# Scaling and biasing the accumulators in the norm stage, and shifting squares and differences between VectorE, ScalarE and GpSimd in an encoder layer

## The chip, the cores and the metric

The kernel runs on one core of one Trainium2 chip. The metric is the device time of one execution in microseconds (us), as the median of several runs. The engines are named as the profile names them: PE is TensorE (matmul), DVE is VectorE, ACT is ScalarE, POOL is GpSimd, SP is SyncE, which issues most of the DMAs. A line number such as L1143 is a line of the kernel before; where the changed kernel's numbers are meant, the text says so.

## What is computed

One encoder layer on 1024 tokens of width 1024, all in fp32. Token mixing (dilated window attention and Fourier mixing, joined by gates) comes first; then a norm, a squared-ReLU MLP of inner width 4096, and a second norm. The part that matters here is:

```python
h = _layer_norm(ALPHA * h + mix, ln1_g, ln1_b)
ff = square(relu(h @ w_up + b_up)) @ w_down + b_down
h = _layer_norm(ALPHA * h + ff, ln2_g, ln2_b)
```

The second sum is `ALPHA * h + b_down + (the down projection's product)`. The first two terms depend on the first norm's output alone, so a kernel is free to form them at any time between the first norm and the last product.

## The kernel before

**Arithmetic.** A number is split into a high part (a cast to fp32r by ACT, L63) and a low part (the difference, by DVE, L64; the function is `split`). A product is three matmuls, high by high, high by low and low by high (`mm3`, L75 to L77). PE therefore has three matmuls of 128x512 for each product, and each operand costs one ACT cast and one DVE difference. The large projections use a scheme of seven block products in place of eight, so the operands are sums and differences of blocks, and the results are joined afterwards.

**Order.** The program is written engine by engine in one Python text; a scheduler with a limited number of buffers for each tag (U 31, wr 3, w 10, S 8, PT 6) decides the order in each engine's queue, and each queue runs strictly in that order. An instruction that waits holds all that is behind it on its engine. `issue_after` keeps a DMA from being issued ahead of another one.

**Norm stage (about 850 to 985 us).** It is the loop over `hf` (two halves of 512 tokens), `c` (two column halves) and `t` (four tiles of 128 tokens). L947 adds the scaled input to the product, L832 to L846 make the statistics, L953 and L954 scale a tile z of 128x1024, and L955 writes it to the DRAM scratch `accd`. Later the tile is transposed by PE (`transposed`, L867), copied out of PSUM by ACT (L872) into `h1t`, and `token_blocks` (L901 to L911) forms the block sums for the up projection on DVE, with ACT casts and DVE differences after each (tiles `tb`).

**Up projection (to about 1276 us).** There are 16 pairs of 128-column blocks; pairs 0 and 1 are done without the block scheme (WHOLE = 2), pairs up to 4 begin early (START = 5). `block_steps` makes the seven products p1 to p7 of a pair. `keep` copies a product out of PSUM (ACT, L976), `joined` adds a second one (DVE, L989), and `done` applies ReLU with the bias on ACT (L980) and then squares: on ACT (L982) for pairs below START, on DVE (L984) for the others. The result q has one of eight S buffers. In p3 four sums and differences of q run on POOL (L1044 to L1050), each followed by a DMA from POOL's queue (L996) to the scratch `qd`; other results go to `qd` from ACT's queue.

**Down projection (about 1276 to 1560 us).** The accumulators `acc` are eight tiles of 128x1024, read back from `accd` (L1133). Eight instructions on DVE (L1135) turn each into ALPHA * acc + b_down; the row b_down is loaded for it (L825, called at L1130). For each of the groups (2,4), (6,4), (10,4) and (14,2) `add_up` goes through seven block products. `a_block` loads a block of q from `qd` into one of three wr buffers (L1139), casts it on ACT (L1141) and forms the low part (L1143); which engine forms it depends on the name of the block and the group:

```python
sub = (nc.vector if name in ("A11", "A12") or pair < WHOLE + 4 and name in ("S2", "S3")
       else nc.gpsimd).tensor_tensor
```

`b_block` forms sums of the weight blocks on DVE (L1163 to L1172) and splits them. `product` runs the matmuls and then adds each PSUM bank into acc on DVE (L1197, the eviction). A bank is used again by a later product, so PE waits for its eviction.

Of the kernel before, what the change touches and what calls it, by code (L numbers as in the profile page):

```python
# [14 lines left out]
ALU = mybir.AluOpType  # L15
# [3 lines left out]
ALPHA = 2 ** 0.25  # L19
# [9 lines left out]
def tile_hybrid_layer(ctx, tc, a, out):  # L29
# [5 lines left out]
    nc = tc.nc  # L35
# [23 lines left out]
    def ps(tag):  # L59
        return psum.tile([128, 512], F32, tag=tag, bufs=PB[tag], name=nm("p" + tag))  # L60
# [586 lines left out]
    for gp in range(2):  # L647
# [5 lines left out]
        for d in range(8):  # L653
# [5 lines left out]
            h, l = cwh[d // 2][:, d % 2], cwl[d // 2][:, d % 2]  # L659
# [162 lines left out]
    def row(name):  # L822
        t = U([128, 1024], name=name)
        src = a[name]
        nc.sync.dma_start(t, bass.AP(tensor=src.tensor, offset=src.offset, ap=[[0, 128], [1, 1024]]))  # L825
        return t
# [22 lines left out]
        nc.vector.tensor_scalar(q[:, 5:6], r, also, None, op0=ALU.mult)  # L849
        return q[:, 0:1], r, q[:, 5:6]  # L850

    g1, b1 = row("ln1_g"), row("ln1_b")
    bup = const.tile([128, 32], F32, name="bup")
    nc.sync.dma_start(bup, a["b_up"])
    accd = dram.tile([8, 128, 1024], F32, name="accd")
# [5 lines left out]
    def transposed(hf, t, h):  # L861
        tc_ = slice(128 * t, 128 * t + 128)
        for q in range(2):
            p = ps("s")
            for i in range(4):
                k = 4 * q + i
                nc.tensor.transpose(p[:, 128 * i:128 * i + 128], h[:, 128 * k:128 * k + 128], ident)  # L867
            for i in range(2):
                dp = 2 * q + i
                if t == 0:  # L870
                    raw[hf, dp] = U([128, 2, 512], name="h1t")
                nc.scalar.copy(  # L872
                    raw[hf, dp][:, :, tc_], p[:, 256 * i:256 * i + 256].rearrange("p (d n) -> p d n", d=2))
        if hf == 0 and t == 3:
            plain_block("B11", 0)
        if hf == 1 and t == 3:
            token_blocks(1)

    def plain_block(name, d0):
        for dp in range(d0, d0 + 2):  # L880
            h_, l_ = U([128, 2, 512], F32R, "tb"), U([128, 2, 512], F32R, "tb")
            split(raw[0, dp], h_, l_)
            for v, x in zip(TB[name], (h_, l_)):
                v.append(x)
# [42 lines left out]
    WHOLE, START = 2, 5  # L927
# [3 lines left out]
    for hf in range(2):  # L931
        zs = [U([128, 1024], name="z") for _ in range(4)]
        stats = []
        for c in range(2):
            s = slice(512 * c, 512 * c + 512)
            w = [weights(a["wout"][c, u], [128, 2, 512]) for u in range(4)]
            for t in range(4):
                p = ps("mm")
                tc_ = slice(128 * t, 128 * t + 128)
                xr = tmp([128, 512])  # L940
                nc.sync.dma_start(xr, a["xr"][512 * hf + 128 * t:512 * hf + 128 * t + 128, s])
                for k in range(8):
                    mm3(p, mgh[hf, k // 2][:, k % 2, tc_], mgl[hf, k // 2][:, k % 2, tc_],
                        w[k // 2][0][:, k % 2], w[k // 2][1][:, k % 2], k == 0, k == 7)
                if len(late) > 1 or late and c == 0:
                    transposed(*late.pop(0))
                nc.vector.scalar_tensor_tensor(zs[t][:, s], xr, ALPHA, p, op0=ALU.mult, op1=ALU.add)  # L947
                if c == 0:
                    stats.append(norm_stats(zs[t], (0,)))
                else:  # L950
                    h = zs[t]
                    mu, r = norm_scale(norm_stats(h, (1,), stats[t]))
                    nc.vector.scalar_tensor_tensor(h, h, mu, g1, op0=ALU.subtract, op1=ALU.mult)  # L953
                    nc.vector.scalar_tensor_tensor(h, h, r, b1, op0=ALU.mult, op1=ALU.add)  # L954
                    nc.sync.dma_start(accd[4 * hf + t], h)  # L955
                    late.append((hf, t, h))


# [1 line left out]
    def block_steps(pair):  # L960
        w = WB[pair]
        ba, bb = bup[:, 2 * pair:2 * pair + 1], bup[:, 2 * pair + 1:2 * pair + 2]
        bank, part = {}, {}

        def product(x, y, b, tag=None):
            first = tag is not None
            if first:
                bank[b] = ps(tag)
            for k in range(4):
                ks = slice(128 * k, 128 * k + 128)  # L970
                h_, l_ = (v[k // 2][:, k % 2] for v in TB[y])
                mm3(bank[b], w[x][:, 0, ks], w[x][:, 1, ks], h_, l_, first and k == 0, k == 3, True)

        def keep(name, b="x", make=tmp):
            part[name] = make([128, 512], name="part")
            nc.scalar.copy(part[name], bank[b])  # L976

        def done(src, bias, r=None):
            r, q = r or tmp([128, 512]), half([128, 512], name="q")
            nc.scalar.activation(r, src, AF.Relu, bias=bias)  # L980
            if pair < START:
                nc.scalar.activation(q, r, AF.Square)  # L982
            else:
                nc.vector.tensor_tensor(q, r, r, op=ALU.mult)  # L984
            return q

        def joined(name, b, bias):
            t = part[name]
            nc.vector.tensor_tensor(t, t, bank[b], op=ALU.add)  # L989
            return done(t, bias, t)  # L990

        pool = nc.gpsimd.tensor_tensor
        q = {}

        def save(name, t):
            (nc.gpsimd if name[0] == "S" else nc.scalar).dma_start(qd[pair - WHOLE, NAMES.index(name)], t)  # L996

        def plain(i, c, t):
            nc.scalar.dma_start(qp[2 * pair + i, :, 512 * c:512 * c + 512], t)

        def whole(c):
            for i, (x, y, bias) in enumerate((("A11", "A12", ba), ("A21", "A22", bb))):
                if c == 0:
                    product(x, "B11", "y", "pt")
                    keep(i, "y", half if pair else tmp)
                    product(y, "B21", "y")
                    plain(i, 0, done(bank["y"], bias))
                else:
                    product(x, "T1", "y", "pt")
                    product(y, "B22", "y")  # L1010
                    plain(i, 1, joined(i, "y", bias))

        def p1():
            product("A11", "B11", "x", "mm")
            keep("r1")

        def p2():
            product("A12", "B21", "y", "pt")
            q[11] = joined("r1", "y", ba)
            save("A11", q[11])  # L1020

        def p6():
            product("S2", "T2", "x")
            keep("r2")

        def p5():
            product("S1", "T1", "z", "s")

        def p7():
            product("S3", "T3", "x")  # L1030
            keep("r3")
            q[22] = joined("r3", "z", bb)
            save("A22", q[22])

        def p4():
            product("A22", "T4", "x")
            q[12] = done(bank["x"], bb)
            save("A12", q[12])

        def p3():  # L1040
            product("S4", "B22", "z")
            q[21] = joined("r2", "z", ba)
            s3 = half([128, 512], name="q")
            pool(s3, q[11], q[21], op=ALU.subtract)  # L1044
            save("S3", s3)
            pool(q[21], q[21], q[22], op=ALU.add)
            save("S1", q[21])
            pool(q[11], q[21], q[11], op=ALU.subtract)
            save("S2", q[11])
            pool(q[12], q[12], q[11], op=ALU.subtract)  # L1050
            save("S4", q[12])

        return dict(c0=lambda: whole(0), c1=lambda: whole(1), p1=p1, p2=p2, p3=p3, p4=p4, p5=p5, p6=p6, p7=p7)
# [73 lines left out]
        r0 = b_raws(WHOLE, 4)  # L1127
    acc = []
    with tc.issue_after(last):
        bdn = row("b_down")  # L1130
        for t in range(8):
            acc.append(U([128, 1024], name="acc"))
            nc.sync.dma_start(acc[t], accd[t])  # L1133
    for t in range(8):
        nc.vector.scalar_tensor_tensor(acc[t], acc[t], ALPHA, bdn, op0=ALU.mult, op1=ALU.add)  # L1135

    def a_block(name, pair):
        r = wr([128, 2, 512])
        load[0] = nc.sync.dma_start(r, qd[pair - WHOLE:pair - WHOLE + 2, NAMES.index(name)].rearrange("b p n -> p b n")).ins  # L1139
        h_, l_ = U([128, 2, 512], F32R), U([128, 2, 512], F32R)  # L1140
        nc.scalar.copy(h_, r)  # L1141
        sub = (nc.vector if name in ("A11", "A12") or pair < WHOLE + 4 and name in ("S2", "S3") else nc.gpsimd).tensor_tensor
        sub(l_, r, h_.bitcast(F32), op=ALU.subtract)  # L1143
        return h_, l_

# [183 lines left out]
```

## Time and profile before

| quantity | value |
| --- | --- |
| median of 3 runs | 1610.8 us (1607.35 to 1611.06) |
| profiled execution | 1611.52 us |
| its span in the profile | 1609.7 us |
| mean granted clock of PE | 0.991 |
| instructions in the span | 20761 |
| read from HBM, written | 159.30 MB, 57.54 MB |
| POOL busy | 268.1 us (17%) |

The profile's span covers the instructions of the engines; the time of the execution has 1.8 us more around it. The profiled execution is 0.7 us above the median. In the profile's groups a line gives engine, operation, output and input tiles, the number of instructions, their busy time and mean length in ns, and after the second bar how long the engine stood idle right before them and for whom. A list of waits gives, for each instruction that waited, the engine and line that it waited for, the total, the number of times and the longest. In the windows the granted clock is the share of full speed that PE was given, and the DMA share is how busy the 16 DMA engines were.

### The profile page before, as it was taken

How to read it: one execution, taken by the hardware profiler on the slowest of the kernel's cores; microseconds unless marked ns; L12 is line 12 of the kernel's file. 1: busy time of each engine (PE TensorE's matmuls, PEld its weight loads, DVE VectorE, ACT ScalarE, POOL GpSimd, SP SyncE). 2: the span in 40 equal slices, each digit the busy share in tenths (PEclk: the TensorE clock that was granted, in tenths of full speed). 3: DMA queues.
4: the chain of work that ended last, by engine and by line, in shares of the span. 5: the costliest groups of instructions: out<-in, count | busy, mean ns of one | idle time of the engine just before them, and what ended most of it. 6: DMA issues, size and time to landing. Idle time of an engine off the chain costs nothing. (4 is left out here: it accounts for less than half of the span.)

```text
span 1609.7 us, 20761 instructions
## 1 busy us (share of the span) xinstructions
PE 1563.2 (97%) x7636; PEld 1274.8 (79%) x7636; DVE 1035.8 (64%) x1708; ACT 647.0 (40%) x1299; POOL 268.1 (17%) x282
## 2 busy tenths in 40 slices
PE   8999999999999999899899999999999989999997
PEld 6788888888988777888788887888888778888885
DVE  7565544144422533947676786477778997878878
ACT  5333334255433645523322355554444443333312
POOL 0000000000100000300000000133333542525414
PEclk9999999999999999999999999999999999999998
DMA  6433333421411232536655533344437763535502
GB/s 187 162 131 110 106 105 121 150 103 54 138 40 61 74 124 75 174 107 186 185 168 161 168 123 131 118 151 146 154 132 261 259 200 124 193 94 170 170 14 92
DMA packets 104224, 218.21 MB, mean 136 GB/s; under 512 B 21128, under 2 KB 30792, under 8 KB 104122
## 3 DMA queue, kind: packets, MB, share of 16 engines
q1 hardware_dynamic: 69498, 167.81, 32.5%
q10 hardware_dynamic: 28320, 27.99, 5.1%
q0 software_dynamic: 6304, 21.07, 3.4%
q8 instruction: 60, 0.98, 0.3%
q14 instruction: 42, 0.34, 0.1%
HBM read 159.30 MB, written 57.54 MB: 135 GB/s over the span
## 5 line engine op out<-in xcount | busy, mean ns | idle before, releaser
L64 DVE TENSOR_TENSOR w<-wr,w 128x1024 fp32r<-128x1024 f32 x59 | 71.9, 1222 | 97.6 <-ACT w L63 85.4
L1143 POOL TENSOR_TENSOR U<-wr,U 128x1024 fp32r<-128x1024 f32 x31 | 88.5, 2868 | 135.8 <-ACT U L1141 87.6
L441 ACT ACTIVATE prob<-prob,st 128x192 f32<-128x192 f32 (+2 forms) x192 | 83.9, 438 | 64.6 <-DVE st L438 53.4
L75 PE MATMUL pmm<-xh,w 128*128 128x512 f32 x256 | 102.0, 398 | 2.9 <-ACT gate L536 2.0
L64 DVE TENSOR_TENSOR wb<-wup,wb 128x512 fp32r<-128x512 f32 x92 | 74.2, 811 | 46.0 <-ACT wb L63 46.0
L63 ACT CAST w<-wr 128x1024 fp32r<-128x1024 f32 x59 | 61.9, 1050 | 102.4 <-PE pmm L76 69.1
L77 PE MATMUL pmm<-xh,w 128*128 128x512 f32 x256 | 102.2, 400 | 0.0
L76 PE MATMUL pmm<-xl,w 128*128 128x512 f32 x256 | 101.9, 398 | 0.0
L63 ACT CAST w<-U 128x1024 fp32r<-128x1024 f32 x49 | 51.2, 1047 | 124.1 <-PE ppt L76 52.3
L1044 POOL TENSOR_TENSOR q<-q,q 128x512 f32<-128x512 f32 x14 | 21.9, 1568 | 474.5 <-ACT q L982 364.9
L63 ACT CAST wb<-wup 128x512 fp32r<-128x512 f32 x92 | 56.4, 623 | 99.0 <-DVE q L984 60.7
L470 POOL MEMSET pt<- 64x128 f32 x80 | 16.0, 200 | 476.0 <-ACT qo L276 269.0
L438 DVE CUSTOM_DVE_ANT_0 prob<-ps,bias 128x192 f32<-128x192 f32 (+2 forms) x192 | 55.8, 348 | 56.7 <-PE ps L430 45.5
L77 PE MATMUL pmm<-tb,wb 128*128 128x512 f32 x224 | 89.3, 398 | 1.3 <-DVE wb L64 1.3
L64 DVE TENSOR_TENSOR wb<-wx,wb 128x512 fp32r<-128x512 f32 x72 | 48.9, 690 | 64.7 <-ACT wb L63 64.5
L75 PE MATMUL pmm<-tb,wb 128*128 128x512 f32 x224 | 89.3, 399 | 0.0
L76 PE MATMUL pmm<-tb,wb 128*128 128x512 f32 x224 | 89.0, 397 | 0.0
L64 DVE TENSOR_TENSOR w<-U,w 128x1024 fp32r<-128x1024 f32 x49 | 81.3, 1660 | 10.3 <-ACT w L63 10.1
L63 ACT CAST wb<-wx 128x512 fp32r<-128x512 f32 x72 | 43.8, 620 | 103.2 <-PE pmm L77 58.2
L1141 ACT CAST U<-wr 128x1024 fp32r<-128x1024 f32 x49 | 50.6, 1045 | 36.7 <-DMA wr<-qd 16.3
L75 PE MATMUL ps<-w,U 128*128 128x512 f32 x144 | 57.6, 400 | 4.1 <-DVE acc L1197 4.1
L77 PE MATMUL pmm<-w,xl 128*128 128x512 f32 x146 | 60.9, 417 | 0.0
(432 smaller groups left out, 4497.4 us busy)
## 6 DMA issues: line engine op xcount, KB each, us to landing
wr<-qd SPq DMA_DIRECT2D x49, 512.0 KB
wup<-in_wup_dram SPq DMA_DIRECT2D x36, 512.0 KB
qd<-q POOLq DMA_DIRECT2D x56, 256.0 KB, 2.7
U<-in_wdn_dram SPq DMA_DIRECT2D x28, 512.0 KB
qd<-q ACTq DMA_DIRECT2D x42, 256.0 KB
wx<-in_wqk_dram SPq DMA_DIRECT2D x19, 512.0 KB
qkd<-qo ACTq DMA_DIRECT2D x32, 256.0 KB
qk<-qkd SPq DMA_DIRECT2D x16, 512.0 KB
```

The lines of the kernel that those rows point to most:

```text
L63: nc.scalar.copy(h, src)
L64: nc.vector.tensor_tensor(l, src, h.bitcast(F32), op=ALU.subtract)
L75: nc.tensor.matmul(o, lh, rh, start=first, stop=False, skip_group_check=on)
L76: nc.tensor.matmul(o, lh, rl, start=False, stop=False, skip_group_check=on)
L77: nc.tensor.matmul(o, ll, rh, start=False, stop=last, skip_group_check=on)
L438: nc.vector.tensor_tensor_reduce(out=e, in0=pp[hh][:, step * i:step * i + n], in1=bias[:, hh, bs], scale=-1.0, scalar=3e38, op0=ALU.add, o ...
L441: nc.scalar.activation(e, e, AF.Exp, bias=m, scale=-1.0, accum_out=st[:, 1, hh, b:b + 1])
L470: nc.gpsimd.memset(t[64 - p0:128 - p0, s], 0.0)
L1044: pool(s3, q[11], q[21], op=ALU.subtract)
L1141: nc.scalar.copy(h_, r)
L1143: sub(l_, r, h_.bitcast(F32), op=ALU.subtract)
```

## The change

Three things change, in one step.

(a) The row b_down is loaded with the rows of the first norm. After the eight transposes of a tile z, DVE forms `z = ALPHA * z + b_down` in place (L874 of the changed kernel), and only then SP writes z to `accd` (L875 there). The eight instructions L1135 and the load of b_down at the start of the down projection are gone; what is read back needs no more work.

(b) The squares of pairs 13 to 15 run on ACT in place of DVE; these are twelve instructions.

(c) All 14 differences of `a_block` for the first group (2,4) run on DVE; six of them (blocks A22, S1 and S4, two each) ran on POOL before.

```diff
-    g1, b1 = row("ln1_g"), row("ln1_b")
+    g1, b1, bdn = row("ln1_g"), row("ln1_b"), row("b_down")
...
                 nc.scalar.copy(
                     raw[hf, dp][:, :, tc_], p[:, 256 * i:256 * i + 256].rearrange("p (d n) -> p d n", d=2))
+        nc.vector.scalar_tensor_tensor(h, h, ALPHA, bdn, op0=ALU.mult, op1=ALU.add)
+        nc.sync.dma_start(accd[4 * hf + t], h)
...
                     nc.vector.scalar_tensor_tensor(h, h, r, b1, op0=ALU.mult, op1=ALU.add)
-                    nc.sync.dma_start(accd[4 * hf + t], h)
                     late.append((hf, t, h))
...
-            if pair < START:
+            if pair < START or pair >= 13:
                 nc.scalar.activation(q, r, AF.Square)
...
     with tc.issue_after(last):
-        bdn = row("b_down")
         for t in range(8):
             acc.append(U([128, 1024], name="acc"))
             nc.sync.dma_start(acc[t], accd[t])
-    for t in range(8):
-        nc.vector.scalar_tensor_tensor(acc[t], acc[t], ALPHA, bdn, op0=ALU.mult, op1=ALU.add)
...
-        sub = (nc.vector if name in ("A11", "A12") or pair < WHOLE + 4 and name in ("S2", "S3") else nc.gpsimd).tensor_tensor
+        sub = (nc.vector if name in ("A11", "A12") or pair < WHOLE + 4 else nc.gpsimd).tensor_tensor
```

PE's instructions keep their order. In the changed kernel the line numbers up to 872 are those of before; then L949, L955 and L956 there are L947, L953 and L954 of before, L983 is L982, L1139 and L1141 are L1141 and L1143, L1167 is L1169, and L1195 is L1197.

The first place is the end of the norm stage on DVE. It begins with the block sums behind the last norm (L901 to L911 before, L903 to L913 after), which the ACT casts and DVE differences (L64, tiles tb) follow; z_7508 is the last of the eight tiles z. Before:

```order
L901 TENSOR_TENSOR t_1342_8023<-h1t_7832,h1t_7823 128x512
L901 TENSOR_TENSOR t_1345_8030<-h1t_7834,h1t_7825 128x512
L902 TENSOR_TENSOR h1t_7823<-h1t_7823,h1t_7423 128x2x256
L902 TENSOR_TENSOR h1t_7825<-h1t_7825,h1t_7425 128x2x256
L907 TENSOR_TENSOR h1t_7423<-h1t_7832,h1t_7823 128x2x256
L907 TENSOR_TENSOR h1t_7425<-h1t_7834,h1t_7825 128x2x256
L64 TENSOR_TENSOR tb_8027<-h1t_7823,tb_8026 128x2x256
L911 TENSOR_TENSOR h1t_7432<-h1t_7432,h1t_7423 128x2x256
L64 TENSOR_TENSOR tb_8034<-h1t_7825,tb_8033 128x2x256
L911 TENSOR_TENSOR h1t_7434<-h1t_7434,h1t_7425 128x2x256
L64 TENSOR_TENSOR tb_8038<-h1t_7832,tb_8037 128x2x256
L901 TENSOR_TENSOR t_1366_8087<-h1t_7832,h1t_7823 128x512
```

After:

```order
L903 TENSOR_TENSOR t_1343_8031<-h1t_7836,h1t_7827 128x512
L903 TENSOR_TENSOR t_1346_8038<-h1t_7838,h1t_7829 128x512
L904 TENSOR_TENSOR h1t_7827<-h1t_7827,h1t_7423 128x2x256
L904 TENSOR_TENSOR h1t_7829<-h1t_7829,h1t_7425 128x2x256
L909 TENSOR_TENSOR h1t_7423<-h1t_7836,h1t_7827 128x2x256
L909 TENSOR_TENSOR h1t_7425<-h1t_7838,h1t_7829 128x2x256
L64 TENSOR_TENSOR tb_8035<-h1t_7827,tb_8034 128x2x256
L913 TENSOR_TENSOR h1t_7432<-h1t_7432,h1t_7423 128x2x256
L64 TENSOR_TENSOR tb_8042<-h1t_7829,tb_8041 128x2x256
L913 TENSOR_TENSOR h1t_7434<-h1t_7434,h1t_7425 128x2x256
L64 TENSOR_TENSOR tb_8046<-h1t_7836,tb_8045 128x2x256
L874 SCALAR_TENSOR_TENSOR z_7508<-z_7508,b_down_7136 128x1024
```

The scaling of the last tile (L874) has come in between two differences of tb; the rest of the piece stands as it did. The other three of the second half stand ahead of this piece: two among the statistics and norms of the last two tiles, and the third right behind the last norm, three rows ahead of the first row shown.

The second place is on DVE in the down projection's first group, before the first eviction of an "s" bank by the third product (acc_10441 before, acc_10449 after: the same accumulator). Before:

```order
L1197 TENSOR_TENSOR acc_10445<-acc_10445,pmm_10615 128x512
L64 TENSOR_TENSOR w_10656<-U_10573,w_10655 128x1024
L1197 TENSOR_TENSOR acc_10447<-acc_10447,po_10629 128x512
L64 TENSOR_TENSOR w_10660<-U_10580,w_10659 128x1024
L1169 TENSOR_TENSOR U_10427<-U_10427,U_10423 128x1024
L1197 TENSOR_TENSOR acc_10441<-acc_10441,ps_10505 128x512
L1169 TENSOR_TENSOR U_10435<-U_10435,U_10431 128x1024
L64 TENSOR_TENSOR w_10729<-U_10427,w_10728 128x1024
```

After:

```order
L1195 TENSOR_TENSOR acc_10453<-acc_10453,pmm_10615 128x512
L1167 TENSOR_TENSOR U_10437<-U_10437,U_10433 128x1024
L1167 TENSOR_TENSOR U_10445<-U_10445,U_10441 128x1024
L1195 TENSOR_TENSOR acc_10455<-acc_10455,po_10629 128x512
L64 TENSOR_TENSOR w_10660<-U_10580,w_10659 128x1024
L1141 TENSOR_TENSOR U_10724<-wr_10721,U_10723 128x1024
L1195 TENSOR_TENSOR acc_10449<-acc_10449,ps_10505 128x512
L64 TENSOR_TENSOR w_10729<-U_10437,w_10728 128x1024
```

The two block sums (L1169 before, L1167 after) no longer enclose the eviction; a difference of `a_block` (L1141) for the fifth block (A22), which POOL made before, stands right ahead of it.

The third place is on ACT near the end of the up projection, between the ReLU of q_10281 (before; q_10291 after) and the copy out of PSUM of part_10349 (part_10359 after). Before:

```order
L980 ACTIVATE part_10043<-part_10043,bup 128x512
L976 COPY part_10305<-pmm_10090 128x512
L980 ACTIVATE PT_10319<-pmm_10075,bup 128x512
L63 CAST w_10497<-U_10427 128x1024
L996 DMA qd<-q_10320 128x512
L1141 CAST U_10467<-wr_10465 128x1024
L976 COPY part_10349<-pmm_10090 128x512
```

After:

```order
L981 ACTIVATE part_10053<-part_10053,bup 128x512
L977 COPY part_10315<-pmm_10100 128x512
L983 ACTIVATE q_10291<-part_10053 128x512
L981 ACTIVATE PT_10329<-pmm_10085,bup 128x512
L63 CAST w_10497<-U_10437 128x1024
L983 ACTIVATE q_10330<-PT_10329 128x512
L1139 CAST U_10467<-wr_10465 128x1024
L997 DMA qd<-q_10330 128x512
L1139 CAST U_10473<-wr_10471 128x1024
L1139 CAST U_10487<-wr_10485 128x1024
L977 COPY part_10359<-pmm_10100 128x512
```

Two squares (L983) have come in, and three casts of `a_block` (L1139) in place of one now stand ahead of the copy of part_10359 (L977).

## The prediction

> **What bounds the kernel now.** I read the busy shares first, then the list of what TensorE (PE) waits for, then the windows around those waits.
>
> The share of busy time from the page, part 1:
>
> ```profile
> PE 1563.2 (97%) x7636; PEld 1274.8 (79%) x7636; DVE 1035.8 (64%) x1708; ACT 647.0 (40%) x1299; POOL 268.1 (17%) x282
> ```
>
> PE is busy for 97% of a span of 1609.7 us, and the change takes no matmul away. It can only win what PE waits or runs slowly. Of the list of PE's waits (us in total, times, longest), these lie where the change acts:
>
> ```profile
> PE ps L75 <- DVE acc L1197: 4.1, 1, 4.1
> ...
> PE ppt L75 <- ACT wb L63: 1.9, 1, 1.9
> PE ps L77 <- DVE U L1143: 1.8, 1, 1.8
> PE pmm L77 <- DVE wb L64: 1.8, 2, 1.3
> ...
> PE ps L75 <- DVE part L989: 1.0, 1, 1.0
> ```
>
> The 4.1, the 1.8 on L1143 and the 1.0 belong to the passage from the up to the down projection (1240 to 1320 us); the other two lie at the end of the norm stage (960 to 985 us). Windows of 40 us give the busy time of PE, PEld, DVE, ACT and POOL with the count of instructions, then the granted clock, the DMA share and GB/s:
>
> ```profile
> 960.00:1000.00 40.00, 36.48 (x144) 28.51 (x144) 27.49 (x44) 25.05 (x44) 0.00 (x0) 0.91 0.30 102
> 1000.00:1040.00 40.00, 40.00 (x174) 32.38 (x173) 21.68 (x33) 20.22 (x34) 1.31 (x2) 1.00 0.38 122
> ...
> 1240.00:1280.00 40.00, 37.15 (x158) 29.21 (x157) 37.53 (x37) 18.10 (x24) 18.00 (x17) 1.00 0.78 274
> 1280.00:1320.00 40.00, 35.73 (x147) 28.07 (x146) 40.00 (x31) 14.16 (x15) 21.08 (x16) 0.96 0.57 183
> ```
>
> A full window holds 174 matmuls, 0.230 us each. The passage's two windows hold 158 and 147: 43 too few, 9.9 us. DVE is busy for 37.5 and 40.0 of 40 us there: it is the late engine. A finer cut of the worst place:
>
> ```profile
> 1305.00:1310.00 5.00, 2.25 (x10) 1.50 (x8) 5.00 (x2) 1.05 (x1) 3.58 (x2) 1.00 0.73 227
> 1310.00:1315.00 5.00, 3.62 (x9) 2.88 (x10) 5.00 (x6) 2.94 (x3) 1.36 (x1) 0.66 0.40 107
> ```
>
> PE stands still from about 1307 to 1311 and then gets 0.66 of its clock for 5 us: 0.34 x 5 = 1.7 us more are lost behind the stall. The timelines of DVE and of POOL say why:
>
> ```profile
> 1307.19 3.45 DVE L1169 TENSOR_TENSOR U<-U,U 128x1024 f32<-128x1024 f32 x1
> 1310.56 0.67 DVE L1197 TENSOR_TENSOR acc<-acc,ps 128x512 f32<-128x512 f32 x1
> 1311.16 1.21 DVE L1169 TENSOR_TENSOR U<-U,U 128x1024 f32<-128x1024 f32 x1
> ```
>
> ```profile
> 1307.15 2.40 POOL L1143 TENSOR_TENSOR U<-wr,U 128x1024 fp32r<-128x1024 f32 x1 [0.97 <-ACT U L1141]
> ```
>
> The eviction that PE waits for (L1197 at 1310.56) stands behind a subtraction of 3.45 us, which takes 1.21 us when it comes again at 1311.16; the long one ran beside a POOL difference.
>
> **The passage, 1240 to 1320.** These groups of DVE, ACT and POOL in that stretch give count, busy us, mean ns and idle before:
>
> ```profile
> L1143 DVE TENSOR_TENSOR U<-wr,U 128x1024 fp32r<-128x1024 f32 x8 | 14.9, 1878 | 0.0
> ...
> L1135 DVE SCALAR_TENSOR_TENSOR acc<-acc,b_down 128x1024 f32<-128x1024 f32 x8 | 12.5, 1572 | 0.8 <-DMA acc<-accd 0.8
> L1141 ACT CAST U<-wr 128x1024 fp32r<-128x1024 f32 x12 | 12.4, 1045 | 17.1 <-DMA wr<-qd 11.6 <-PE pmm L77 4.0 <-PE ppt L77 1.4
> ...
> L984 DVE TENSOR_TENSOR q<-part 128x512 f32<-128x512 f32 x7 | 7.5, 1066 | 1.7 <-issue 1.7
> ...
> L984 DVE TENSOR_TENSOR q<-PT 128x512 f32<-128x512 f32 x3 | 3.1, 1043 | 0.0
> ```
>
> Off DVE go the eight scalings, 12.5 us, and ten of the twelve squares, 7.5 + 3.1 = 10.6 us (two lie ahead of the stretch). On DVE come six differences at 1.21 us, 7.3 us, if nothing stretches them; at the mean of 1.88 us of their eight like they are 11.3 us. DVE falls from 37.5 + 40.0 = 77.5 us to between 61.7 and 65.7 of 80. Ahead of the late eviction stand two of the six, so at that place at least 23.1 - 2 x 3.4 = 16 us of work have gone, against a lateness of 4.1 us. The squares of 1231 to 1240 go as well, and POOL has no difference of the first group left to stretch DVE with (its L1143 falls from 31 to 25). So I expect all three waits to go, 1.0 + 1.8 + 4.1 = 6.9 us, with the slow clock behind the longest, 1.7 us: 8.6 us by the waits, 9.9 us by the missing matmuls. I take the middle, 9.3, and keep both as bounds.
>
> What is late next there is ACT. It gains twelve squares; its own square costs, in the norm stage,
>
> ```profile
> L982 ACT ACTIVATE q<-PT 128x512 f32<-128x512 f32 x4 | 2.6, 640 | 0.0
> ```
>
> so 7.7 us more on an engine busy for 18.1 + 14.2 of 80 us. By sum that is covered. By order it is close in one place: a square on ACT writes one of eight q buffers, so it has to wait until POOL has read the old content, and three casts and a copy from PSUM stand behind it. The places on ACT, POOL and PE today:
>
> ```profile
> 1262.93 0.58 ACT L976 COPY part<-pmm 128x512 f32<-128x512 f32 x1
> ```
>
> ```profile
> 1257.44 1.36 POOL L1046 TENSOR_TENSOR q<-q,q 128x512 f32<-128x512 f32 x1
> 1259.10 0.56 POOL L996 DMA_DIRECT2D qd<-q  x1 [0.30 <-POOL q L1046]
> ```
>
> ```profile
> 1264.40 0.39 PE L75 MATMUL pmm<-tb,wb 128*128 128x512 f32 x1
> ```
>
> If POOL's L1046 still ends at 1258.8, the square ends at 1259.4, three casts of 1.05 (L1141 above) at 1262.6 and the copy at 1263.2; PE writes that bank again at 1264.40. That is 1.2 us to spare: covered, at zero, but thinly. POOL has no reason to be later, since its operands come from ACT at once and not from the queue on DVE. The eight reads of accd now bring rows that are already scaled; the 512 KB of b_down no longer go over the queue in this stretch.
>
> **The norm stage, 880 to 985.** The eight scalings come here, each on 128x1024 after the eight transposes of its tile. The nearest like it, and the three windows of the end (columns as above):
>
> ```profile
> L954 DVE SCALAR_TENSOR_TENSOR z<-z,lnq,ln_b 128x1024 f32<-128x1024 f32 x5 | 6.4, 1283 | 0.1
> ```
>
> ```profile
> 960.00:970.00 10.00, 9.64 (x42) 7.53 (x42) 9.56 (x16) 8.47 (x17) 0.00 (x0) 1.00 0.00 1
> 970.00:980.00 10.00, 6.84 (x25) 4.94 (x24) 9.28 (x16) 7.34 (x13) 0.00 (x0) 0.85 0.37 136
> 980.00:990.00 10.00, 10.00 (x37) 7.95 (x36) 4.71 (x7) 4.29 (x7) 0.00 (x0) 0.81 0.59 200
> ```
>
> ```profile
> 910.26 2.36 DVE L64 TENSOR_TENSOR tb<-h1t,tb 128x1024 fp32r<-128x1024 f32 x2 [6.48 <-ACT tb L63]
> ...
> 958.43 0.69 DVE L64 TENSOR_TENSOR tb<-h1t,tb 128x512 fp32r<-128x512 f32 x1 [2.80 <-ACT tb L63]
> 959.04 0.68 DVE L911 TENSOR_TENSOR h1t<-h1t,h1t 128x512 f32<-128x512 f32 x1
> 960.44 0.69 DVE L64 TENSOR_TENSOR tb<-h1t,tb 128x512 fp32r<-128x512 f32 x1 [0.72 <-ACT tb L63]
> ```
>
> The first half's four scalings, 5.1 us, stand around the idle 6.48 us before 910.26, and PE has no wait on a norm there: zero, and if that cover failed, 1.28 us for each. The second half's four, again 5.1 us, stand in the dense piece up to 980, where DVE's idle time is 2.80 + 0.72 = 3.5 us. So 5.1 - 3.5 = 1.6 us reach the end, where PE waits for ACT and DVE (1.9 and 1.3). Bounds: zero if the transposes' copies hide the rest, 5.1 us if the two gaps can't be used. The granted clock adds a term of its own: 0.85 and 0.81 of 10 us are 1.5 + 1.9 = 3.4 us lost today, and no single wait there is above 1.9 us. Moving the waits by 1.6 us can take that loss away (down to -3.4) or add half as much (+1.7); I take it as unchanged. The Trainium skill, "TensorE: Matmul & The Clock Gate", section "HAM oscillation — how this bites in real kernels", asks only for no idle gap of PE above about 3.4 us; by that rule the clock would not fall here at all and a longer wait would cost its own length. The 0.85 and 0.81 after waits of at most 1.9 us speak against the rule as a safe bound, so the +1.7 stays in the range.
>
> The stores of accd move from the norm to behind the scalings and SP's count stays the same. A z buffer comes free only when its store has landed; page part 6 gives a store from another queue:
>
> ```profile
> qd<-q POOLq DMA_DIRECT2D x56, 256.0 KB, 2.7
> ```
>
> The DMA share is 0.00 from 960 to 970, so I take it as hidden; its price in the open is 2.7 us.
>
> **The sum.** -9.3 + 1.6 = -7.7 us from the profiled run of 1611.5 us: 1603.8. That run lies 0.7 us above the median of the three, so 1603.1 against it: 1603. The likeliest case itself runs from -9.9 + 1.6 - 3.4 = -11.7 (1599.1) to -8.6 + 1.6 + 1.7 = -5.3 (1605.5). A measurement of this kernel can tell about 0.3%, 4.8 us, from no change, so faster means below 1606.0 and slower above 1615.6.
>
> **Rivals.** *ACT takes DVE's place in the passage (0.15).* If POOL lets go of the q buffer more than 1.2 us later than today, the casts and the copy come late to PE. Two steps of POOL (1.36 and 0.30 + 0.56 for the issue, 2.2 us each) are 4.5 us, 3.3 of them seen by PE, and with the slow clock 5.0. For it: POOL's steps follow one another without a gap, and the square is in ACT's queue ahead of casts. Against: POOL starts earlier. Time: 1603 + 5.0 = 1608, no change that can be told.
>
> *The eviction stays late (0.07).* All differences are now on DVE, and each needs a cast that needs a load into one of three wr buffers; ACT waited 11.6 us for those loads. An eviction queued behind such a difference waits for the load. The Trainium skill, "SBUF — State Buffer", section "Who interferes with whom", adds that a VectorE instruction with two inputs in SBUF is held up by a GpSimd instruction that reads SBUF, which the new differences can meet while POOL forms its sums (the 3.45 us row agrees). Then the 4.1 and 1.7 us remain: 9.3 - 5.8 - 1.6 = 1.9 us won, 1609. Against: buffers come free earlier once DVE has 14 us or more of idle time.
>
> *The norm stage outweighs it (0.06), slower.* Place: the end of the norm stage. DVE is at 9.56 and 9.28 of 10 there and PE waits for it already. If the gaps of 2.80 and 0.72 can't be used (5.1 us) and ACT's next cast waits for the store of the last z (2.7), PE stands 7.8 us more; at about 1.7 us of slow clock for each 2 us of waiting that is 14.4 us, less 9.3: +5.1, 1616. It is slower than before from about 5 us of new waiting on. Against: DMA is empty there and the transposes of PE, not DVE, end the 2.80.
>
> **How the numbers follow.** The likeliest case has 0.72, the rivals 0.15, 0.07 and 0.06. Faster takes 0.72 and a quarter of ACT's case (one step of POOL late, not two): 0.76; same 0.18; slower 0.06. The range runs from 1599.5 to 1608.0: it leaves out some of the gain of the clock below, the late eviction and the slower case above.
>
> **What would show it.** PE's list of waits should have no row of DVE on acc, U or part between 1240 and 1320, and both 40 us windows should hold 170 or more matmuls at a clock of 1.00. DVE should show idle time in every 10 us from 1260 on. Around 975 to 985 PE should wait 1 to 2 us more. A wait of PE for ACT's copy near 1264 would show the first rival; the acc row still there, the second; PE below 130 matmuls from 960 to 1000, the third. If all three waits are gone and the time is still above 1606, the prediction is wrong in its belief that the waits are the time.

## The result and the profile after

The changed kernel takes 1603.0 us (median of 8 runs, 1600.5 to 1605.4) against 1613.4 us for the kernel before (8 runs). The ratio is 0.9942 with a 95% interval of 0.9930 to 0.9955, so the change is worth 0.58% or 9.4 us. The forecast was 1603 with a gain of 7.7 us. The five runs of the kernel before that were taken after the first three took 1612.9 to 1614.7 us, the first three 1607.4 to 1611.1, so the ratio is the better number.

The windows of the profile after, with the columns of before (PE, PEld, DVE, ACT, POOL, granted clock, DMA share, GB/s), for the end of the norm stage, the piece after it, and the passage:

```profile
960.00:1000.00 40.00, 35.44 (x141) 27.59 (x140) 29.91 (x48) 24.73 (x45) 0.00 (x0) 0.91 0.35 125
1000.00:1040.00 40.00, 40.00 (x174) 32.42 (x173) 21.10 (x33) 20.08 (x34) 0.00 (x0) 1.00 0.39 125
...
1240.00:1280.00 40.00, 40.00 (x174) 32.45 (x173) 26.53 (x24) 25.22 (x35) 18.68 (x21) 1.00 0.89 321
1280.00:1320.00 40.00, 40.00 (x174) 32.41 (x174) 38.71 (x38) 17.04 (x17) 9.38 (x10) 1.00 0.63 215
```

The passage holds 174 + 174 = 348 matmuls where it held 158 + 147 = 305: 43 more, 9.9 us, all of what was missing, at full clock. The norm stage holds 141 where it held 144: 0.7 us lost. The two together are 9.2 us, close to the 9.4 of the ratio. What PE waits for at the end of the norm stage:

```profile
PE ppt L75 <- ACT wb L63: 2.0, 1, 2.0
PE pmm L77 <- DVE wb L64: 1.7, 1, 1.7
PE ppt L75 <- ACT PT L981: 0.9, 1, 0.9
```

That is 4.6 us against 0.4 + 1.9 + 1.3 = 3.6 before. In the passage there is no wait of PE for DVE on acc, U or part any more. The timeline of DVE ahead of the eviction, and PE's matmul behind it:

```profile
1300.31 1.21 DVE L64 TENSOR_TENSOR w<-U,w 128x1024 fp32r<-128x1024 f32 x1
1301.45 1.21 DVE L1141 TENSOR_TENSOR U<-wr,U 128x1024 fp32r<-128x1024 f32 x1
1302.58 0.67 DVE L1195 TENSOR_TENSOR acc<-acc,ps 128x512 f32<-128x512 f32 x1
```

```profile
1305.35 0.39 PE L75 MATMUL ps<-w,U 128*128 128x512 f32 x1
```

The eviction ends at 1303.25 and PE comes for the bank at 1305.35: 2.1 us to spare, with every DVE instruction in front at 1.21 us. The margin is small: DVE is busy for the whole 10 us in each of three windows around it:

```profile
1280.00:1290.00 10.00, 10.00 (x45) 8.09 (x45) 10.00 (x8) 4.27 (x5) 8.72 (x9) 1.00 0.46 174
1290.00:1300.00 10.00, 10.00 (x44) 8.07 (x43) 10.00 (x11) 4.04 (x5) 0.66 (x2) 1.00 0.60 176
1300.00:1310.00 10.00, 10.00 (x45) 8.11 (x44) 10.00 (x11) 3.89 (x4) 0.00 (x0) 1.00 0.46 143
```

### The profile page after: what moved, and what is told of

It is laid out like the page before. It is cut to its first block, busy times and chain, and to the rows that moved or that the text cites. A ratio compares the mean times of both kernels' runs of the same rounds, so it can differ in the third digit from the quotient of the medians.

```text
span 1601.4 us, 20756 instructions
## 1 busy us (share of the span) xinstructions
PE 1559.2 (97%) x7636; PEld 1273.1 (80%) x7636; DVE 1022.2 (64%) x1702; ACT 653.7 (41%) x1311; POOL 249.2 (16%) x276
## 4 chain that ended last, share of the span: by engine, by line
PE 51%; DVE 5%; DMA 1%; ACT 0%; issue 0%; SPq 0%; DVEq 0%; ACTq 0%
PE pmm L75 8%; PE pmm L77 8%; PE pmm L76 8%; PE ps L75 5%; PE ps L77 5%; PE ps L76 5%; PE ppt L77 3%; PE ppt L75 3%; PE ppt L76 3%; DMA wg<-ad 1%; DVE acc L1221 1%; DVE tb L64 1%; PE po L77 1%; PE po L75 1%; PE po L76 1%; DVE lnst L832 0%
## 5 line engine op out<-in xcount | busy, mean ns | idle before, releaser
L64 DVE TENSOR_TENSOR w<-wr,w 128x1024 fp32r<-128x1024 f32 x59 | 71.8, 1221 | 98.1 <-ACT w L63 85.9
L64 DVE TENSOR_TENSOR wb<-wup,wb 128x512 fp32r<-128x512 f32 x92 | 77.1, 843 | 45.1 <-ACT wb L63 42.7
L1141 POOL TENSOR_TENSOR U<-wr,U 128x1024 fp32r<-128x1024 f32 x25 | 72.6, 2917 | 145.4 <-ACT U L1139 101.4
L64 DVE TENSOR_TENSOR w<-U,w 128x1024 fp32r<-128x1024 f32 x49 | 81.0, 1655 | 20.7 <-ACT w L63 10.6
L1045 POOL TENSOR_TENSOR q<-q,q 128x512 f32<-128x512 f32 x14 | 18.3, 1309 | 474.8 <-ACT q L983 384.9
L64 DVE TENSOR_TENSOR wb<-wx,wb 128x512 fp32r<-128x512 f32 x72 | 48.9, 689 | 63.9 <-ACT wb L63 63.8
L75 PE MATMUL pmm<-w,xh 128*128 128x512 f32 x146 | 60.8, 419 | 0.6 <-ACT w L63 0.6
L75 PEld LDWEIGHTS pmm<-xh,w 128*128 128x128 f32 x256 | 48.9, 191 | 15.5 <-ACT gate L536 3.5
```

The costliest lines, as they stand in the source:

```text
L64: nc.vector.tensor_tensor(l, src, h.bitcast(F32), op=ALU.subtract)
L75: nc.tensor.matmul(o, lh, rh, start=first, stop=False, skip_group_check=on)
```

## The experiments

Two theories stood against each other. The **queue theory** is the one in the prediction: PE waits for as long as DVE's queue is behind, so any DVE work taken off ahead of the eviction shortens the wait. The **lock theory**: DVE's instructions with two SBUF inputs are held up while a POOL instruction reads SBUF, and what counts is whether such a meeting lies ahead of the eviction. All ratios are to runs of the kernel before on the same chip. "Matmuls" is the count in the two windows from 1240 to 1320 in one profile of each kernel (before 305, full 348); one is 0.230 us. A difference of 5 matmuls between two profiles is within what profiles of the same code show (last section).

| kernel | ratio, 95% interval | matmuls | long acc wait |
| --- | --- | --- | --- |
| whole change | 0.9942 (0.9930 to 0.9955) | 348 | none |
| (a) alone | 1.0026 (1.0013 to 1.0038) | 295 | 8.1 |
| (b) alone | 0.9987 (0.9976 to 0.9997) | 310 | 3.6 |
| (c) alone | 0.9960 (0.9947 to 0.9972) | 324 | none |
| (a) and (b) | 0.9972 (0.9960 to 0.9983) | 326 | 3.6 |
| (a) and (c) | 0.9952 (0.9935 to 0.9969) | 337 | none |
| (b) and (c) | 0.9955 (0.9939 to 0.9971) | 335 | none |

**(a) alone (a_only).** The norm stage and the acc lines as in the change, the other two lines as before:

```diff
-            if pair < START or pair >= 13:
+            if pair < START:
...
-        sub = (nc.vector if name in ("A11", "A12") or pair < WHOLE + 4 else nc.gpsimd).tensor_tensor
+        sub = (nc.vector if name in ("A11", "A12") or pair < WHOLE + 4 and name in ("S2", "S3") else nc.gpsimd).tensor_tensor
```

> Part (a) alone: the scalings move to the norm stage, squares and differences stay as before. Queue theory (PE's stalls in the passage are the length of DVE's queue since its last idle time at 1257.9): the lateness there is 1.0 + 1.8 + 4.1 = 6.9 us, and the scalings that stood behind 1257.9 are 1.96 + 2.82 + 2.35 + 1.21 = 8.3 us, so all three waits go and the slow clock with them: -9.3, plus 0.7 for the norm stage, about -8.6 us against before. Lock theory (only DVE's stretched instructions beside POOL's differences matter): the 4.1 us wait and its slow clock stay, the two small waits go, about -2.8 + 0.7 = -2 us.

It is slower than before, by 0.26%. PE's longest wait, and the timelines of DVE and POOL around it (L1166 and L1169 are the block sums, L1194 the eviction, L1140 the difference in this kernel's numbers; two instructions of one kind share a row):

```profile
PE ps L75 <- DVE acc L1194: 8.1, 1, 8.1
```

```profile
1299.29 6.45 DVE L1166 TENSOR_TENSOR U<-U,U 128x1024 f32<-128x1024 f32 x2
1305.67 0.67 DVE L1194 TENSOR_TENSOR acc<-acc,pmm 128x512 f32<-128x512 f32 x1
1306.27 2.35 DVE L1169 TENSOR_TENSOR U<-U,U 128x1024 f32<-128x1024 f32 x2
1308.54 0.67 DVE L1194 TENSOR_TENSOR acc<-acc,po 128x512 f32<-128x512 f32 x1
1309.13 6.26 DVE L64 TENSOR_TENSOR w<-U,w 128x1024 fp32r<-128x1024 f32 x2
1315.32 1.27 DVE L1194 TENSOR_TENSOR acc<-acc,ps 128x512 f32<-128x512 f32 x2
```

```profile
1298.92 5.75 POOL L1140 TENSOR_TENSOR U<-wr,U 128x1024 fp32r<-128x1024 f32 x2 [7.83 <-issue]
1308.68 5.64 POOL L1140 TENSOR_TENSOR U<-wr,U 128x1024 fp32r<-128x1024 f32 x2 [4.01 <-DVE U L1169]
```

Eight scalings have left the passage and the wait has grown from 4.1 to 8.1 us. Four POOL differences, two at a time, run beside the two pairs of DVE instructions that take 6.45 and 6.26 us; between them, with POOL idle, the same kind of pair takes 2.35. The meetings cost DVE 12.7 - 4.7 = 8.0 us, ahead of the eviction. In the profile before they cost some 6.1 us there, 2.2 of them in the 3.45 us row of the prediction and the rest in two rows ahead of it, whose like take 2.35 (two) and 1.21 us with POOL idle:

```profile
1297.63 4.55 DVE L1143 TENSOR_TENSOR U<-wr,U 128x1024 fp32r<-128x1024 f32 x2
...
1304.44 2.83 DVE L64 TENSOR_TENSOR w<-U,w 128x1024 fp32r<-128x1024 f32 x1
```

The scheduler has also drawn the two L1169 ahead of the eviction, which adds 2.3 us that stood behind it before (L1172 there). The queue theory, in the form "less DVE work, less waiting", fails here. The lock theory, as it was put down, did not foresee this either: it had the long wait stay at 4.1 us and a gain of 2 us in all. Nor do both small waits go: the one on U does, the one on part grows from 1.0 to 2.0 us.

**(b) alone (b_only).** Only `pair < START or pair >= 13` is taken over.

> Part (b) alone: twelve squares move from DVE to ACT. Queue theory: behind 1257.9 there were 1.77 + 0.68 + 0.68 + 0.68 + 1.78 = 5.6 us of squares, so 6.9 - 5.6 = 1.3 us of waiting remain, at full clock: about -7.3 us. Lock theory: the two small waits go and the long one stays: about -3 us.

0.13% faster, some 2 us: 310 matmuls are 5 more than before, 1.2 us. The long wait stays at 3.6 us, as the lock theory has it. Both theories had the small ones go; the one on U nearly does, the one on part grows from 1.0 to 2.1 us:

```profile
PE ps L75 <- DVE acc L1197: 3.6, 1, 3.6
...
PE ps L75 <- DVE part L989: 2.1, 2, 1.6
...
PE ps L77 <- DVE U L1143: 0.3, 1, 0.3
```

**(c) alone (c_only).** Only the line `sub = ...` is taken over.

> Part (c) alone: the first group's six POOL differences move to DVE. Queue theory: DVE is rid of about 2.1 + 1.6 + 2.2 = 5.9 us of stretching beside POOL and takes on two differences (2.4 us) ahead of the late eviction, so 3.5 of the 6.9 us go; the waits of 1.0 and 1.8 stay since they lie ahead of POOL's first difference: about -3.5 us, and -1.7 more if the wait that is left is too short for the slow clock (-5.2). Lock theory: the long wait goes entirely: -5.8 us, with the same two small waits left.

0.40% faster, some 6.5 us. The long wait and the slow clock behind it are gone, although DVE has two differences more ahead of the eviction and all scalings and squares; the two small waits stay:

```profile
PE ps L77 <- DVE U L1143: 1.8, 1, 1.8
...
PE ps L75 <- DVE part L989: 1.5, 1, 1.5
```

324 matmuls are 19 more, 4.4 us: 27 more behind 1280, and 8 fewer ahead of it, where the granted clock is now 0.96 (before 1.00). Another 1.2 us come from the norm stage, whose code is unchanged (last section). So (c) alone is the largest part. The time alone does not decide between the theories, which had 5.8 and 3.5 to 5.2 us; that no wait is left at the eviction speaks for the lock theory.

**(b) and (c) (bc), (a) and (b) (ab), (a) and (c) (ac).** Each leaves out one part.

> Parts (b) and (c) without (a): the scalings stay at the start of the down projection. Queue theory: 5.6 + 3.5 = 9.1 us of DVE go against a lateness of 6.9, all waits go and the norm stage costs nothing: -8.6 to -9.9 us, as fast as the whole change or up to 1 us faster. If the scalings in the passage were needed for the gain, 3 us or more of waiting would be left and it would be at least 3 us slower than the whole change.

> Parts (a) and (b) without (c): POOL keeps six differences of the first group, DVE has neither scalings nor the twelve squares. After the first four runs the queue theory stands against a lock theory: a DVE instruction with two SBUF inputs is held up for the length of a POOL difference that it meets, so what counts is whether such a meeting stands right ahead of the eviction that PE waits for, not how much DVE has to do. Lock: an acc wait of 3 to 8 us stays (a alone had 8.1), time within 4 us of before. Queue: 8.3 + 5.6 = 13.9 us of DVE work have gone against 6.9 of lateness, no acc wait, about -9 us.

> Parts (a) and (c) without (b): the squares of pairs 13 to 15 stay on DVE. Both theories let the long wait go, since POOL has no difference of the first group. If (b) has no share of its own, it is as fast as the whole change (-9 us against before). If the squares are what makes the two small waits at 1268 and 1275, 1.0 + 1.8 us of them stay and it is 2 to 3 us slower than the whole change (-6.5).

Without (a), 13 matmuls are missing (3.0 us): bc wins 6.9 us in the passage where the queue theory gave 8.6 to 9.9, so the scalings are not free there. A part wait of 1.8 us stays. Without (c), 22 are missing (5.1 us), most of it in one acc wait of 3.6 us and the slow clock behind it, though 13.9 us of DVE work have gone; by its ratio ab is 4.5 us faster than before, a little more than the 4 that the lock theory allowed. Without (b), 11 are missing (2.5 us): a part wait of 2.0 us stays. By the ratios, whose intervals overlap, leaving out (a) or (b) can't be told from the whole change; leaving out (c) can. The counts set all three apart from it. In this table and before, every kernel with only one of (a) and (b), or neither, keeps a part wait of 1.0 to 2.1 us; the two with both, ab and the whole change, have none. What a part is worth depends on the others: alone (a) loses 2.3 us in the passage (10 matmuls), as the last one it wins 3.0.

**POOL reads with nothing behind them (pool_reads).** The whole change, and POOL reads more; nobody uses what it writes:

```diff
         sub(l_, r, h_.bitcast(F32), op=ALU.subtract)
+        if pair < WHOLE + 4 and name in ("A22", "S1", "S4"):
+            for e in range(2):
+                v = h_[:, e].bitcast(F32)
+                nc.gpsimd.tensor_tensor(half([128, 512], name="idle"), v, v, op=ALU.subtract)
```

> The whole change, and in addition POOL subtracts the high part of each of the six blocks from itself into a spare buffer that nobody reads, in two instructions of 128x512 for each block (twelve in all). DVE's instructions and their order are those of the whole change. Lock theory: DVE's two-input instructions that meet these are held up, 1.3 us each, several in 1295 to 1315 take 2.3 to 2.6 us instead of 1.21, the slack of 2.1 us at the eviction goes and PE waits there again for 0.5 to 4 us. Queue theory: DVE's work has not changed, so its times stay at 1.21 us and so does the kernel's time.

PE's wait for the eviction is back, and the same DVE instructions in the same order are longer (L1170 block sums, L1140 differences, L1198 evictions):

```profile
PE ps L75 <- DVE acc L1198: 2.6, 2, 1.8
```

```profile
1296.26 3.52 DVE L1170 TENSOR_TENSOR U<-U,U 128x1024 f32<-128x1024 f32 x2
1299.70 0.67 DVE L1198 TENSOR_TENSOR acc<-acc,po 128x512 f32<-128x512 f32 x1
1300.30 1.78 DVE L64 TENSOR_TENSOR w<-U,w 128x1024 fp32r<-128x1024 f32 x1
1302.01 2.06 DVE L1140 TENSOR_TENSOR U<-wr,U 128x1024 fp32r<-128x1024 f32 x1
1303.99 0.68 DVE L1198 TENSOR_TENSOR acc<-acc,ps 128x512 f32<-128x512 f32 x1
1304.59 1.46 DVE L64 TENSOR_TENSOR w<-U,w 128x1024 fp32r<-128x1024 f32 x1
1305.97 2.06 DVE L1140 TENSOR_TENSOR U<-wr,U 128x1024 fp32r<-128x1024 f32 x1
```

```profile
1295.68 3.02 POOL L1144 TENSOR_TENSOR idle<-U 128x512 f32<-128x512 f32 x2 [3.88 <-ACT U L1138]
1299.96 3.02 POOL L1144 TENSOR_TENSOR idle<-U 128x512 f32<-128x512 f32 x2 [1.26 <-ACT U L1138]
1303.25 3.70 POOL L1144 TENSOR_TENSOR idle<-U 128x512 f32<-128x512 f32 x2 [0.26 <-ACT U L1138]
```

L1140 takes 2.06 in place of 1.21 us, less than the 2.3 to 2.6 expected, and the two windows hold 335 matmuls in place of 348 (3.0 us). DVE has no more work than in the whole change, so this is the lock by itself. The two evictions (0.67 and 0.68, one input from PSUM) keep their length. The total moves by less than the interval can tell (0.9953 against 0.9942).

**POOL writes without reading (pool_writes).** The same place, but memsets:

```diff
+        if pair < WHOLE + 4 and name in ("A22", "S1", "S4"):
+            for e in range(6):
+                nc.gpsimd.memset(half([128, 512], name="idle"), 0.0)
```

> The whole change, and in addition 36 POOL memsets of 128x512 into spare buffers that nobody reads, behind POOL's last sums of the up projection (four of them stand between those sums). They write SBUF and read none. If only POOL's reads hold DVE up, DVE's differences and block sums between 1290 and 1320 stay at 1.21 us, no acc wait comes, and the time is that of the whole change within 2 us. If any use of SBUF by POOL holds DVE up, they stretch as in pool_reads (1.46 to 2.3 us) and an acc wait of 1 us or more comes back.

The ratio is 0.9935 (0.9912 to 0.9959) and the passage is full (175 + 175 records). POOL writes for 15 us without a pause, and DVE beside it is not touched (L1169 block sums, L1140 differences in this kernel's numbers):

```profile
1292.50 15.09 POOL L1143 MEMSET idle<- 128x512 f32 x32
```

```profile
1297.16 1.22 DVE L1140 TENSOR_TENSOR U<-wr,U 128x1024 fp32r<-128x1024 f32 x1
...
1298.89 2.35 DVE L1169 TENSOR_TENSOR U<-U,U 128x1024 f32<-128x1024 f32 x2
...
1302.90 1.22 DVE L1140 TENSOR_TENSOR U<-wr,U 128x1024 fp32r<-128x1024 f32 x1
```

So neither POOL's being busy nor its writing holds DVE up; its subtractions, which read SBUF, do. Whether a POOL instruction that reads one tensor and not two does the same was not tried.

**The price of the norm stage (half_scaled, twice, late_scale, late_scale_again).** half_scaled keeps the second half's scalings in the passage:

```diff
+        if hf == 0:
+            nc.vector.scalar_tensor_tensor(h, h, ALPHA, bdn, op0=ALU.mult, op1=ALU.add)
...
+        bdn2 = row("b_down")
...
+    for t in range(4, 8):
+        nc.vector.scalar_tensor_tensor(acc[t], acc[t], ALPHA, bdn2, op0=ALU.mult, op1=ALU.add)
```

> The whole change, but only the first half's four scalings in the norm stage; the second half's four stand at the start of the down projection as before. If the norm stage's price is the second half's scalings, PE's waits at 968 to 985 fall back to those of before (0.4 + 1.9 + 1.3, about 0.7 us less than with the whole change). In the passage DVE gets 4 x 1.21 = 4.9 us more; it was idle for 7 us between 1250 and 1270, so by sum they are hidden and the kernel is 0.7 us faster than the whole change (-9 to -10 against before). If the rows land too late for the idle time, the slack of 2.1 us at the eviction is used up and 1 to 3 us of waiting come back.

The norm stage's waits are those of before (1.9 and 1.3), as expected; the passage has 166 + 174 = 340 matmuls, 8 fewer than the whole change (1.8 us), with a part wait of 1.6 us back. The ratio, 0.9944 (0.9926 to 0.9963), is that of the whole change: the norm stage gains 8 matmuls (149 against 141), the passage loses 8. Of the gain, 5 are the clock that c_only gets without an edit there (last section), so by its waits the norm stage gains 1.0 us.

twice adds two scalings for each tile of the second half:

```diff
+        if hf:
+            nc.vector.scalar_tensor_tensor(h, h, 1.0, bdn, op0=ALU.mult, op1=ALU.subtract)
+            nc.vector.scalar_tensor_tensor(h, h, 1.0, bdn, op0=ALU.mult, op1=ALU.add)
         nc.vector.scalar_tensor_tensor(h, h, ALPHA, bdn, op0=ALU.mult, op1=ALU.add)
```

> The whole change, and for each tile of the norm stage's second half two more scalings of 128x1024 on DVE (subtract and add b_down, which leaves z as it was but for rounding): eight more, 8 x 1.21 = 9.7 us. With the whole change DVE has no idle time left from 938 to 982, so if the price of a scaling is its own length once the gaps are used up, PE's waits at 968 to 985 grow by about 9.7 us and the whole kernel with them; the slow clock, on by about 1.7 us for each 2 us of waiting, may add up to 8 us more: slower than the whole change by 10 to 18 us, slower than before by 1 to 9. If other waits hide it, it costs under 5 us.

The ratio is 1.0002 (0.9988 to 1.0016): the whole gain is gone. Against the whole change that is some 9.7 us, a little under the range of 10 to 18, and against before 0.3 us, not the 1 to 9 expected. The norm stage in its profile:

```profile
920.00:960.00 40.00, 38.64 (x183) 31.36 (x182) 36.22 (x62) 16.16 (x36) 0.00 (x0) 1.00 0.32 111
960.00:1000.00 40.00, 27.08 (x94) 20.50 (x93) 30.80 (x48) 20.75 (x38) 0.00 (x0) 0.79 0.33 119
```

94 matmuls against 141, and 183 against 191 in the window ahead of it (the whole change had 191 there): 55 fewer, 12.7 us. PE's waits from 900 to 1000 are 14.4 us against 4.6, so 9.8 us of this are waiting, for 9.7 us of DVE work, and 2.9 are the slow clock, where the expectation had up to 8. The count is more than the 9.7 us of the ratios, which are known to about 3 us; in the two profiles, stages far ahead of the edits make up for part of it: from 760 to 800 the whole change has 167 matmuls, twice 177 and before 181. So a scaling too many here costs its own length, and by the count up to a third more for the slow clock.

late_scale writes the second half's scalings after the up projection's first pair:

```diff
+        if hf == 0:
+            scaled()
+        else:
+            rest_scale.append(scaled)
...
     steps[1]["c0"]()
+    for f in rest_scale:
+        f()
```

> The whole change, but the second half's four scalings are written after the up projection's first pair; the scheduler then puts the last two of them behind the last block sums, just ahead of the differences that PE waits for at the end. If what counts is DVE work ahead of those differences, nothing is won (within 1 us of the whole change). If the order within the piece counts, the waits at 968 to 985 shift by up to 1.2 us either way and the slow clock by up to 3.4.

> The kernel late_scale once more, with more rounds, to see whether it beats the whole change. Its first profile had the norm stage and the passage take as long as with the whole change (one wait of 4.5 us in place of several that add up to 5.1), so if nothing but the order in the norm stage differs, its ratio to before is that of the whole change, 0.994, within 0.002. If the single wait is really cheaper, the ratio stays at 0.992 with an interval that lies below 0.9935.

The first time its ratio was 0.9919 (0.9889 to 0.9949), the second time, with more runs, 0.9940 (0.9923 to 0.9956): that of the whole change. PE's waits of 4.6 us in all (not 5.1, as the expectation has it) become one of 4.5 us and one of 0.7. No kernel tried is faster than the whole change beyond the intervals.

## Why the prediction was right, point by point

**The time and the waits.** Right: all three DVE waits of the passage went, with the slow clock. The middle that was taken, 9.3 us, is a little low; the count of missing matmuls, 9.9, was the better of the two bounds. That 1603 was met to the microsecond is luck: the gain was 1.7 us larger than forecast (9.4), and the median of the kernel before 2.6 us above that of the three runs from which the forecast was reckoned.

**The norm stage.** The mechanism was right and the size too large: 1.6 us in the sum, 0.7 by the missing matmuls and 1.0 by the waits. The kernels with (a) in the norm stage as here have waits of 4.3 to 4.6 us there, those without it 3.6. DVE's gaps of 2.80 and 0.72 us are closed in the profile after, so the cover was used as described; the row names an ACT cast as what ended the 2.80, not the transposes, as the third rival has it. The loss to the slow clock was taken as unchanged, and it is (0.91 in both).

**ACT.** Right that it stays hidden. The square in question waited 0.28 us for POOL, and PE did not wait for the copy, which itself waited for PE:

```profile
1260.21 0.63 ACT L983 ACTIVATE q<-PT 128x512 f32<-128x512 f32 x1 [0.28 <-POOL q L1047]
...
1263.88 0.59 ACT L977 COPY part<-pmm 128x512 f32<-128x512 f32 x1 [0.20 <-PE pmm L77]
```

POOL's step ended at 1260.18, 1.4 us later than in the profile before (1258.80), which is more than the 1.2 us to spare. It stayed hidden because PE too came later: it writes that bank again at 1266.46 in place of 1264.40, 2.0 us behind the end of the copy. In (b) alone, too, PE waits for no ACT instruction in the passage, so no run here shows this rival.

**The reason given for the long wait failed in part.** The step "at least 23.1 - 2 x 3.4 = 16 us of work have gone, against a lateness of 4.1 us" treats DVE's busy time as work that can be taken off anywhere. a_only takes 12.5 us off and waits 8.1; ab takes off 13.9 us behind the last idle time and waits 3.6. DVE's time ahead of the eviction contains what the POOL differences that it meets add to it, and in a_only freeing DVE moved these meetings and made them dearer (8.0 us against 6.1). The prediction saw the stretched 3.45 us row and named the end of such rows, but gave that no size. The sum came out right because (c), which it valued at 7.3 us more work against the stretching saved, takes these meetings away. It is worth 5.1 us as the last part and 4.4 alone, the most of the three. The Trainium skill, "SBUF — State Buffer", section "Who interferes with whom", says that a VectorE instruction with two SBUF inputs contends with a GpSimd instruction that reads SBUF and not with one that only writes it; pool_reads (1.21 to 2.06 us) and pool_writes (1.22 beside memsets) agree with both halves. The prediction used that rule against the change, as part of the second rival; here it was the main reason for it.

**"DVE should show idle time in every 10 us from 1260 on"** was wrong: from 1280 to 1310 it is busy throughout, and the eviction is 2.1 us ahead of PE, not the 12 that the sum would give.

**The slower rival** has its price from twice: there PE waits 14.4 us at the end of the norm stage against 3.6 before, and the time is that of before, where the rival had about 5 us of new waiting undo the gain. Its slow-clock term, 1.7 us for each 2 us of waiting, was nearly three times too large: by the count, 9.8 us of waiting more than in the whole change brought 2.9.

## What to carry to other kernels

Busy time of DVE beside a POOL that reads SBUF is not DVE's own work: before summing what a change takes off, count a long row at the length that the same instruction has with POOL idle. Where PE waits for a PSUM eviction, look at the two or three rows ahead of it on its engine and move whatever locks or waits there; work taken off elsewhere may only shift the meeting, as with (a) alone. The parts of this change don't add: they give -10, +5 and +19 matmuls alone and +43 together.

## What the runs showed of the hardware

The same waits do not always bring the same loss of clock. The norm stage of half_scaled has the waits of before (1.9, 1.3 and 0.4 us) and still runs 149 matmuls in the window where before has 144:

```profile
960.00:1000.00 40.00, 36.48 (x149) 28.54 (x149) 28.78 (x46) 26.46 (x47) 0.00 (x0) 0.96 0.30 106
```

The clock is 0.96 in place of 0.91, half as much loss. c_only, whose code there is that of before, has the same waits and also 0.96 and 149; (b) alone and bc, whose code there is the same too, have 0.91 with 143 and 144. A closer cut, before and then c_only:

```profile
977.10:979.40 2.30, 1.22 (x3) 1.02 (x4) 2.23 (x4) 1.81 (x3) 0.00 (x0) 0.50 0.76 265
```

```profile
977.10:979.40 2.30, 0.72 (x2) 0.30 (x2) 2.25 (x5) 1.46 (x3) 0.00 (x0) 1.00 0.41 125
```

In windows of 0.2 us the granted clock is 0.50 from 977.0 to 983.8 us in the profile of before and from 979.4 to 982.9 in that of c_only, and 1.00 on both sides of these: 6.8 us of half clock against 3.4. The slow clock behind the long wait of before lasts 3.4 us too (0.34 x 5 = 1.7 us lost), and that behind the 8.1 us of a_only about 10.2, three times as long. So in these stretches the slow clock comes in pieces of 3.4 us at half clock. What decides between one piece and two for the same waits, when they fall perhaps, no run here shows. The difference is 5 matmuls, 1.2 us, which no edit made; single profiles of this kernel should not be compared more finely.

A POOL memset of 128x512 took 0.47 us (32 in 15.09 us) against 1.5 to 2.0 us for a POOL subtraction of that shape beside DVE in pool_reads.
